# A bidirectional hybrid encoder layer on one core: strided moving operands of the dilated attention are copied by ScalarE into contiguous tiles first

## The chip, the core and the metric

The kernel is written for Trainium2 and runs on one core of one chip. The metric is device time in microseconds, as the median of several runs; the profile is one further execution under the hardware profiler. The core has five engines, each with its own instruction stream that it works through in order: PE (TensorE, the matrix multiplier; its weight loads are shown apart as PEld), DVE (VectorE), ACT (ScalarE), POOL (GpSimd) and SP (SyncE, which issues most DMAs). They wait for each other by semaphores.

## The reference, cut to what matters

One post-norm encoder layer over 2048 tokens of width 1024. Three mixers read one input projection: A, attention over dilated windows with 6 heads of 64; B, multi-head latent attention with 6 heads; C, chunked spatial gating. Their outputs are normalised and projected, and a squared-ReLU MLP follows. The change touches A alone:

```python
DILATED_PATTERNS = ((128, 1), (512, 4), (2048, 16))      # window, dilation

def _dilated_band_attention(q, k, v, window, dil, slopes):
    band = window // (2 * dil)                            # 64 for every pattern
    ...                                                   # tokens r, r+dil, r+2*dil, ... form one sequence
    s = jnp.einsum('brhnqc,brhnkc->brhnqk', qs, kw).astype(jnp.float32) * (Dh ** -0.5)
    bias = -(slopes[:, None, None, None] * (dil * jnp.abs(off)).astype(jnp.float32))
    s = jnp.where(valid, s + bias, NEG_INF)
    m = s.max(-1, keepdims=True)
    p = jnp.exp(s - m)
    den = p.sum(-1, keepdims=True)
    o = jnp.einsum('brhnqk,brhnkc->brhnqc', (p / den).astype(v.dtype), vw)
    ...
```

The three patterns of a head are then combined by the softmax of their log-sums.

## The kernel before, in words

The program has three parts: the latent columns of the input projection, a mixed part in which the latent attention `latent()` of B runs while "fillers" are woven into it one after the other, and the feed-forward. The fillers are `projection()`, then `dilated()` (its first matmul stands at 715.5 us of the profiled execution, its last value matmul at 1343.5 us), then the output projection. The loop in `mixers` decides by rates how many steps of a filler come after each step of `latent()`; inside that the framework's scheduler orders every engine's instructions for itself, by its own model of their durations and by priorities. So the order in which an engine works is fixed when the program is built.

A step of `latent()` is one 128-key tile of one block of 512 queries: three score matmuls of 512 columns into a bank `st` (L611 to L613), two exponentials of it on ACT (`pr` L618 and `ph` L619), a difference on POOL (`pl` L621), a sum on DVE (`ac` L636), and four steps later two value matmuls into `av` (L643, L644). A maximum runs ahead of it: matmul `mx` L593 and its reduction on DVE, L594. The three PSUM banks `st` are shared with the scores of `dilated()`, the four banks `mx` with its maxima and its sums.

`dilated()` treats head after head. `QA`, `QB`, `KA` and `KB` hold queries and keys of one head with the tokens along the free axis, in float32r, 4 bytes each. For dilation d the tokens of one residue lie d elements apart, so that the function `tok` cuts a slice with step 4 (pattern p = 1) or 16 (p = 2); for p = 0 it is contiguous. Per head there are 16 tiles of 128 tokens for each pattern, grouped in 20 units: 8 of p = 0, 8 of p = 1 (two tiles each) and 4 of p = 2 (four tiles each). For a tile three matmuls run: one for the maximum, a unit ahead for the next head (`amx`, L865: weights from QA, moving operand from KA), and two for the score (`ast`, L938 and L939: weights from KA and KB, moving operand from QA and QB). Both the weights and the moving operand are cut with the step. The moving operand has 256 columns, except that of the fourth tile of a unit of p = 2, which has 128. The maxima are read by DVE (`jk`, L870), the scores get their bias on DVE (`tt`, L947 to L961), an exponential on ACT (`apr`, L964), and a value matmul two units later (`aav`, L995).

The scheduling of `dilated()` has these constants: `D_LAG` = 2 (value matmuls two units behind the scores), `D_MAX` and `D_MRATE` (2.2 units of maxima for the next head with each score unit, from the fourth on), and priorities `HP`.

Of the kernel before, what the change touches and what calls it, by code (L numbers as in the profile page):

```python
# [12 lines left out]
F32 = mybir.dt.float32  # L13
F32R = mybir.dt.float32r
# [20 lines left out]
DILS = (1, 4, 16)  # L35
BIG = 1e30
OFFX = 60
RB = 3
ME = 3
LLAG = 4  # L40
U_STEP = 1
# [38 lines left out]
HP_DE = 0  # L80
HP_DV = 100
HP_DC = 0
HP = dict(L=HP_L, PG=HP_PG, PW=HP_PW, PE=HP_PE, LS=HP_LS, LE=HP_LE, LP=HP_LP, LM=HP_LM, LA=HP_LA, LV=HP_LV, LF=HP_LF, LQ=HP_LQ, LK=HP_LK, DM=HP_DM, DR=HP_DR, DS=HP_DS, DT=HP_DT, DE=HP_DE, DV=HP_DV, DC=HP_DC)
MS_C = None
MS_M = None
MS_F = None
# [13 lines left out]
def hybrid_layer(ctx: ExitStack, tc: tile.TileContext, a):  # L100
# [651 lines left out]
    def dilated():  # L752
# [3 lines left out]
        fp = sbuf(es, "af")  # L756
        dp = es.enter_context(tc.tile_pool(name="ad", bufs=2, space=DRAM))

        D = fp.tile([P, 256], F32, name="D")
        dma(D, a["dist"])  # L760

        KB = fp.tile([65, S], F32R, name="KB")
        pool.memset(f(KB[64:65]), 1.0)
# [1 line left out]
        def prep(h):  # L765
            hp, o = h // 2, (h % 2) * 64
            rows = slice(o, o + 64)
            s = dict(h=h)
            QA = qp.tile([P, S], F32R, tag="QA", name=f"QA{h}")
            QB = qp.tile([65, S], F32R, tag="QB", name=f"QB{h}")  # L770
            KA = qp.tile([P, S], F32R, tag="KA", name=f"KA{h}")
            s.update(QA=QA, QB=QB, KA=KA, KB=KB, V=[], bias=[])

            def load(c):
                cs_ = slice(c * 1024, (c + 1) * 1024)
                dma(QA[0:64, cs_], qa_d[hp][0][rows, cs_])
                dma(KA[0:64, cs_], ka_d[hp][0][rows, cs_])
                dma(QA[64:128, cs_], qa_d[hp][0][rows, cs_])
                dma(KA[64:128, cs_], ka_d[hp][1][rows, cs_])
                dma(QB[0:64, cs_], qa_d[hp][1][rows, cs_])  # L780

            s["parts"] = [lambda: load(0), lambda: load(1)]

            def rest():
                for p, d in enumerate(DILS):
                    bt = qp.tile([P, 256], F32, tag=f"bias{p}", name=f"bias{h}_{p}")
                    act.activation(bt, D, AF.Copy, scale=-8.0 * SLOPES[h] * d)
                    s["bias"].append(bt)
            s["parts"].insert(0, rest)

            def values(p):
                d = DILS[p]
                v = qp.tile([P, d, NT // d, 66], F32, tag=f"v{p}", name=f"v{h}_{p}", bufs=1)
                src = va_d[:, h * HD:(h + 1) * HD].rearrange("(n p r) c -> p r n c", r=d, p=P)
                pool.memset(v[:, :, :, 64:65], 1.0)
                for r in range(d if d == 4 else 1):
                    if d == 16:
                        dma(v[:, :, 0, 0:64], src[:, :, 0])
                    else:
                        dma(v[:, r, :, 0:64], src[:, r])  # L800
                s["V"].append(v.rearrange("p r n c -> p (r n) c")[:, :, 0:65])
            s["values"] = values
            s["mc"] = qp.tile([P, 3, 16], F32, tag="mc", name=f"mc{h}")
            s["u"] = 0
            return s

        def tok(ap, d, r, i0, n):
# [12 lines left out]
            return min(w0, S // DILS[p] - 256), 256, (j * pitch, j * pitch + 256)  # L820

        def cols(ap, p, tl, j):
            r, n, w0, w, o = tl[j]
            m0, m, (c0, c1) = wide(p, tl, j)
            if p == 2 and c1 - c0 > P:
                return ap.rearrange("p (i r) -> p r i", r=16)[:, r:r + 2, :]
            return tok(ap, DILS[p], r, m0, m)

        def bank_cols(ps, p, tl, j):
            m0, m, (c0, c1) = wide(p, tl, j)  # L830
            out = ps[:, c0:c1]
            return out.rearrange("p (r i) -> p r i", i=P) if p == 2 and c1 - c0 > P else out

        def at(p, tl, j):

# [18 lines left out]
                units.append((p, ts_[u:u + g], u))  # L854
        NU = len(units)

        def max_to(s, lim):
            while s["u"] < lim:
                u = s["u"]
                p, tl, base = units[u]  # L860
                d = DILS[p]
                ps = bank("mx", f"amx{s['h']}_{u}")
                with hp("DM"):
                    for j, (r, n, w0, w, o) in enumerate(tl):
                        pe.matmul(bank_cols(ps, p, tl, j), tok(s["QA"], d, r, n * P, P),  # L865
                                  cols(s["KA"], p, tl, j), start=True, stop=True, skip_group_check=True)
                    for j, (r, n, w0, w, o) in enumerate(tl):
                        col = {0: n, 1: n * 4 + r, 2: r}[p]
                        jk = ep.tile([P, 256], BF16, tag="jk", name=f"jk{s['h']}_{u}_{j}", bufs=1)
                        dve.tensor_tensor_reduce(jk[:, :w], ps[:, at(p, tl, j):at(p, tl, j) + w], s["bias"][p][:, o:o + w],  # L870
                                                 1.0, -3e38, ALU.add, ALU.max, s["mc"][:, p, col:col + 1])
                s["u"] = u + 1
                if s["u"] == NU:
                    max_done(s)
# [54 lines left out]
        def score(s, u):  # L929
            p, tl, base = units[u]  # L930
            d = DILS[p]
            h = s["h"]
            nm = f"{h}_{u}"
            st = bank("st", f"ast{nm}")
            with hp("DS"):
                for j, (r, n, w0, w, o) in enumerate(tl):
                    o_ = bank_cols(st, p, tl, j)
                    pe.matmul(o_, tok(s["KA"], d, r, n * P, P), cols(s["QA"], p, tl, j), start=True, stop=False, skip_group_check=True)  # L938
                    pe.matmul(o_, tok(s["KB"], d, r, n * P, P), cols(s["QB"], p, tl, j), start=False, stop=True, skip_group_check=True)  # L939
            tt = ep.tile([P, TB], F32, tag="tt", name=f"tt{nm}", bufs=2)  # L940
            pr = ep.tile([P, TB], F32, tag="pr", name=f"apr{nm}", bufs=D_LAG + 1)
            with hp("DT"):
                b = s["bias"][p]
                ws = [e[3] for e in tl]
                if p == 2:
                    rng = [(0, TB)]
                    dve.tensor_tensor(tt.rearrange("p (j w) -> p j w", w=P), st.rearrange("p (j w) -> p j w", w=P),  # L947
                                      b[:, None, 64:192].to_broadcast([P, 4, P]), op=ALU.add)
                elif ws == [256, 256]:
                    rng = [(0, TB)]  # L950
                    dve.tensor_tensor(tt.rearrange("p (j w) -> p j w", w=256), st.rearrange("p (j w) -> p j w", w=256),
                                      b[:, None, :].to_broadcast([P, 2, 256]), op=ALU.add)
                else:
                    rng = []
                    for j, (r, n, w0, w, o) in enumerate(tl):
                        x0 = at(p, tl, j)
                        if rng and rng[-1][1] == x0:
                            rng[-1] = (rng[-1][0], x0 + w)
                        else:
                            rng.append((x0, x0 + w))  # L960
                        dve.tensor_tensor(tt[:, x0:x0 + w], st[:, x0:x0 + w], b[:, o:o + w], op=ALU.add)  # L961
# [765 lines left out]
```

## Time and profile before

| | us |
|---|---|
| median of 3 runs (2996.32 to 3002.77) | 3000.21 |
| the profiled execution, by the same clock as the runs | 3006.01 |
| its span, from the first to the last instruction | 3004.2 |
| PE busy in the span | 2827.7 |
| DVE busy | 2149.7 |
| POOL busy | 1664.1 |
| ACT busy | 1332.7 |

The profiled execution is 5.8 us above the median. Each engine's busy time is the time in which at least one of its instructions was being worked on. Matmuls overlap: of a row that is shown with 0.40 us, the next one starts 0.23 us later, so what a matmul costs PE is read from the distance of two starts, not from its own duration. PEclk is the clock that PE was granted, as a share of full speed.

### The profile page before, as it was taken

To read this page: it belongs to the slowest core of one execution; us is meant where nothing else is said; L and a number is where in the kernel's file an instruction comes from. 1 tells how busy PE (TensorE), PEld (TensorE's weight loads), DVE (VectorE), ACT (ScalarE), POOL (GpSimd) and SP (SyncE) were. 2 spreads that over 40 slices of the span, in tenths; PEclk is the share of its full clock that TensorE was granted. 3 is DMA by queue.
4 is the path that set the end of the run, shared out by engine and by line. 5 is a ranking of instruction groups with operands and counts; after the bars stand their busy time and mean duration, and the time that the engine had idled before them with its cause. 6 is when DMAs were issued, how large, how long until landed. Compare 5 with 4: busy or idle time off the path is not lost. (4 is left out here: it accounts for less than half of the span.)

```text
span 3004.2 us, 38216 instructions
## 1 busy us (share of the span) xinstructions
PE 2827.7 (94%) x12556; PEld 2293.6 (76%) x12556; DVE 2149.7 (72%) x3519; ACT 1332.7 (44%) x2504; POOL 1664.1 (55%) x1251
## 2 busy tenths in 40 slices
PE   9999899999989999998999899989999999999996
PEld 7776777887777788886777688868887777777774
DVE  4246899887878988888867633383336777778899
ACT  4325555566544555465544434343434332222333
POOL 0115556567744554468755444454445765556667
PEclk9999999999999999998999999999999999999998
DMA  5345334236032444114365533333335322222222
GB/s 167 126 137 167 109 107 132 90 107 130 14 66 43 87 85 84 29 40 130 93 199 159 159 106 112 109 119 109 106 112 196 103 84 74 84 82 78 80 71 95
DMA packets 267760, 314.00 MB, mean 105 GB/s; under 512 B 91804, under 2 KB 157980, under 8 KB 267036
## 3 DMA queue, kind: packets, MB, share of 16 engines
q1 hardware_dynamic: 254248, 295.82, 33.0%
q10 hardware_dynamic: 13312, 15.73, 1.5%
q8 instruction: 99, 1.62, 0.2%
q14 instruction: 101, 0.83, 0.1%
HBM read 209.72 MB, written 98.60 MB: 103 GB/s over the span
## 5 line engine op out<-in xcount | busy, mean ns | idle before, releaser
L621 POOL TENSOR_TENSOR pl<-pr,ph 128x512 fp32r<-128x512 f32 x384 | 556.8, 1463 | 353.4 <-ACT ph L619 233.8
L636 DVE TENSOR_TENSOR ac<-ac,pr 128x512 f32<-128x512 f32 x312 | 359.2, 1151 | 45.4 <-ACT pr L618 38.3
L1571 DVE TENSOR_TENSOR acc<-o,acc 128x512 f32<-128x512 f32 x416 | 275.2, 683 | 110.6 <-PE o L151 108.4
L618 ACT ACTIVATE pr<-st 128x512 f32<-128x512 f32 x384 | 228.4, 597 | 232.0 <-PE st L613 209.2
L594 DVE TENSOR_REDUCE m<-mx 128x1 f32<-128x512 f32 x384 | 253.9, 681 | 40.3 <-PE mx L593 39.2
L619 ACT ACTIVATE ph<-st 128x512 fp32r<-128x512 f32 x384 | 224.0, 596 | 41.4 <-PE av L643 31.5
L643 PE MATMUL av<-ph,VV 128*128 128x512 f32 x384 | 161.2, 420 | 14.3 <-DVE y L658 14.3
L611 PE MATMUL st<-QH,KL 96*128 96x512 f32 x384 | 162.3, 423 | 12.1 <-ACT ph L619 12.1
L644 PE MATMUL av<-pl,VV 128*128 128x512 f32 x384 | 163.4, 426 | 6.0 <-POOL pl L621 5.5
L593 PE MATMUL mx<-KH,QH 96*128 96x512 f32 x384 | 157.5, 435 | 5.2 <-DVE m L594 1.9
L612 PE MATMUL st<-QL,KH 96*128 96x512 f32 x384 | 157.6, 410 | 0.0
L613 PE MATMUL st<-QH,KH 97*128 97x512 f32 x384 | 157.2, 412 | 0.0
L1499 DVE TENSOR_TENSOR t<-t,h 128x512 f32<-128x512 f32 x32 | 22.0, 686 | 142.8 <-PE h L151 132.0
L995 PE MATMUL aav<-apr,v 128*65 128x128 f32 (+3 forms) x624 | 115.5, 329 | 1.9 <-DVE mc L870 1.8
L870 DVE CUSTOM_DVE_ANT_0 jk<-amx,bias 128x256 bf16<-128x256 f32 (+2 forms) x288 | 103.3, 359 | 12.2 <-PE amx L865 4.6
L938 PE MATMUL ast<-QA,KA 128*128 128x256 f32 (+1 forms) x288 | 105.5, 371 | 4.6 <-DVE tt L961 4.3
L995 PEld LDWEIGHTS aav<-apr,v 128*65 128x65 f32 x624 | 82.5, 143 | 31.5 <-issue 2.7
L149 PE MATMUL po<-woh,y 128*128 128x512 f32 x256 | 103.8, 407 | 0.6 <-DVE xt L1310 0.3
L964 ACT ACTIVATE apr<-tt 128x192 f32<-128x192 f32 (+2 forms) x180 | 77.3, 467 | 60.9 <-PE aav L995 39.1
L150 PE MATMUL po<-woh,y 128*128 128x512 f32 x256 | 101.8, 399 | 1.7 <-DVE y L1233 1.7
L151 PE MATMUL po<-wol,y 128*128 128x512 f32 x256 | 100.6, 396 | 2.5 <-DVE wol L1192 2.5
L939 PE MATMUL ast<-QB,KB 65*128 65x256 f32 (+1 forms) x288 | 102.7, 368 | 0.0
(9014 smaller groups left out, 8722.6 us busy)
## 6 DMA issues: line engine op xcount, KB each, us to landing
A<-in_w SPq DMA_DIRECT2D x128, 256.0 KB, 2.7
hid_d<-t SPq DMA_DIRECT2D x128, 256.0 KB, 2.1
A<-hid_d SPq DMA_DIRECT2D x128, 256.0 KB, 3.0
B<-in_w_ff SPq DMA_DIRECT2D x64, 256.0 KB, 4.5
xr<-in_xT SPq DMA_DIRECT2D x56, 256.0 KB, 2.9
wr<-in_wf SPq DMA_DIRECT2D x48, 256.0 KB, 3.7
yr<-y_d SPq DMA_DIRECT2D x64, 128.0 KB, 2.5
xt<-in_x SPq DMA_DIRECT2D x32, 256.0 KB, 3.3
```

Of the source, the lines that this page charges most:

```text
L593: pe.matmul(ps, s["QH"][0:96, qt * P:(qt + 1) * P], kh[0:96, kc * TB:(kc + 1) * TB], start=True, stop=True)
L594: dve.tensor_reduce(s["m16"][:, qt, kc:kc + 1], ps, AX.X, ALU.max)
L611: pe.matmul(st, kl[0:96, kk], s["QH"][0:96], start=True, stop=False)
L612: pe.matmul(st, kh[0:96, kk], s["QL"][0:96], start=False, stop=False)
L618: act.activation(pr, st, AF.Exp, scale=SC)
L619: act.activation(ph, st, AF.Exp, scale=SC)
L621: pool.tensor_tensor(pl, pr, f(ph), op=ALU.subtract)
L636: (pool if kt in AC_POOL else dve).tensor_tensor(s["ac"], s["pr"] if kt == 1 else s["ac"], pr, op=ALU.add)
L643: pe.matmul(s["av"], VV[h][:, kt], ph, start=(kt == 0), stop=False)
L644: pe.matmul(s["av"], VV[h][:, kt], pl, start=False, stop=(kt == NT - 1))
L995: pe.matmul(s[key][0:65, c0:c0 + w], s["V"][p][:, units[u][2] + j], pr[:, a0:a0 + w], start=(first[key] == i), stop=(last[key] == i), skip ...
L1571: dve.tensor_tensor(t, ps, t, op=ALU.add)
```

## The change

Before a unit of p = 1 or p = 2 is computed, ScalarE copies the strided slice that serves as the moving operand into a contiguous tile of 512 columns (`straight`). One such tile holds one residue of p = 1 (which serves two units) or four residues of p = 2 (one unit). For the maxima it is the keys, `kc`, in one buffer (`KCB` = 1), copied when the first unit that needs it is emitted. For the scores it is the queries, `qac` and `qbc`, in two buffers each (`QCB` = 2), copied one unit ahead. The weights are still cut with the step from QA, KA and KB. That is 8 groups x 3 copies x 6 heads = 144 copies of 512 columns. To make room in SBUF, the value tiles of the three patterns share one tag with two buffers, the bias tiles are filled by a DMA for each head instead of from a resident tile `D` (and are half as wide for p = 2), and `RB` falls from 3 to 2 (the tiles `arb` that carry the reciprocals at the end of a head).

```diff
-RB = 3
+RB = 2
...
+KCB = 1
+QCB = 2
...
-                    bt = qp.tile([P, 256], F32, tag=f"bias{p}", name=f"bias{h}_{p}")
-                    act.activation(bt, D, AF.Copy, scale=-8.0 * SLOPES[h] * d)
+                    w0, w1 = (64, 192) if p == 2 else (0, 256)
+                    bt = qp.tile([P, w1 - w0], F32, tag=f"bias{p}", name=f"bias{h}_{p}")
+                    dma(bt, a["dist"][:, w0:w1])
+                    act.activation(bt, bt, AF.Copy, scale=-8.0 * SLOPES[h] * d)
...
-                v = qp.tile([P, d, NT // d, 66], F32, tag=f"v{p}", name=f"v{h}_{p}", bufs=1)
+                v = qp.tile([P, NT, 66], F32, tag="v", name=f"v{h}_{p}").rearrange("p (r n) c -> p r n c", r=d)
...
+        def straight(ap, p, g, tag, nm, bufs):
+            t = ep.tile([ap.shape[0], TB], F32R, tag=tag, name=nm, bufs=bufs)
+            if p == 1:
+                src, dst = tok(ap, 4, g, 0, TB), t
+            else:
+                src, dst = ap.rearrange("p (i r) -> p r i", r=16)[:, 4 * g:4 * g + 4], t.rearrange("p (r i) -> p r i", r=4)
+            act.copy(dst, src)
+            return t
...
+        def keys_of(s, u):
+            p = units[u][0]
+            g = group(p, u)
+            if g is not None and s.get("kg") != (p, g):
+                s["kg"] = p, g
+                with hp("DK"):
+                    s["kc"] = straight(s["KA"], p, g, "kc", f"kc{s['h']}_{u}", KCB)
+
+        def queries_of(s, u):
+            p = units[u][0]
+            g = group(p, u)
+            if g is not None and (p, g) not in s["qc"]:
+                with hp("DQ"):
+                    s["qc"][p, g] = (straight(s["QA"], p, g, "qa", f"qac{s['h']}_{u}", QCB),
+                                     straight(s["QB"], p, g, "qb", f"qbc{s['h']}_{u}", QCB))
...
+                keys_of(s, u)
...
-                        pe.matmul(bank_cols(ps, p, tl, j), tok(s["QA"], d, r, n * P, P),
-                                  cols(s["KA"], p, tl, j), start=True, stop=True, skip_group_check=True)
+                        pe.matmul(dst_cols(ps, p, tl, j), tok(s["QA"], d, r, n * P, P),
+                                  piece_of(s["kc"], p, tl, j) if p else cols(s["KA"], p, tl, j), start=True, stop=True, skip_group_check=True)
...
+            queries_of(s, u)
+            if u + 1 < NU:
+                queries_of(s, u + 1)
...
-                    pe.matmul(o_, tok(s["KA"], d, r, n * P, P), cols(s["QA"], p, tl, j), start=True, stop=False, skip_group_check=True)
-                    pe.matmul(o_, tok(s["KB"], d, r, n * P, P), cols(s["QB"], p, tl, j), start=False, stop=True, skip_group_check=True)
+                    qa, qb = ([piece_of(t, p, tl, j) for t in s["qc"][p, group(p, u)]] if p else
+                              [cols(s[t], p, tl, j) for t in ("QA", "QB")])
+                    pe.matmul(o_, tok(s["KA"], d, r, n * P, P), qa, start=True, stop=False, skip_group_check=True)
+                    pe.matmul(o_, tok(s["KB"], d, r, n * P, P), qb, start=False, stop=True, skip_group_check=True)
```

The scheduler orders the program anew from the second half of the projection to the start of the output projection; ahead of it and behind it every engine's instructions stand as they stood. Two places show what comes to lie between what.

PE, maxima of the first head, the units 15 to 17 (p = 1 ends with unit 15, p = 2 begins with 16). The last two numbers of a name are unit and buffer; `amx` are maxima, `st` scores and `av` values of the latent attention. Before:

```order
L865 MATMUL amx_15_7142<-KA_6750,QA_6748 128x256 x2
L611 MATMUL st_2_5_7405<-QH_2_6405,KL_1896 128x512
L612 MATMUL st_2_5_7405<-QL_2_6406,KH_1895 128x512
L613 MATMUL st_2_5_7405<-QH_2_6405,KH_1895 128x512
L865 MATMUL amx_16_7164<-KA_6750,QA_6748 128x256 x3
L865 MATMUL amx_16_7164<-KA_6750,QA_6748 128x128
L865 MATMUL amx_17_7177<-KA_6750,QA_6748 128x256 x3
L865 MATMUL amx_17_7177<-KA_6750,QA_6748 128x128
```

And in the changed program:

```order
L903 MATMUL amx_15_7151<-kc_14_7142,QA_6746 128x256 x2
L648 MATMUL av_1_6964<-pl_1_15_7296,VV_4832 128x512
L615 MATMUL st_2_5_7422<-QH_2_6405,KL_1896 128x512
L616 MATMUL st_2_5_7422<-QL_2_6406,KH_1895 128x512
L617 MATMUL st_2_5_7422<-QH_2_6405,KH_1895 128x512
L903 MATMUL amx_16_7175<-kc_16_7173,QA_6746 128x256 x3
L903 MATMUL amx_16_7175<-kc_16_7173,QA_6746 128x128
L903 MATMUL amx_17_7190<-kc_17_7188,QA_6746 128x256
```

The matmuls are the same, but each group of maxima now reads a `kc` of its own, and since there is one buffer, the copy of the next `kc` has to lie between the last `amx` of one group and the first of the next. Four matmuls of 512 columns stand between units 15 and 16, and none between 16 and 17.

ACT, maxima of the third head and scores of the second, from the exponentials of unit 12 (`apr_12`) to those of the latent attention's step 5 (`pr_0_5`). Before:

```order
L964 ACTIVATE apr_12_8241<-tt_12_8240 128x192
L964 ACTIVATE apr_12_8241<-tt_12_8240 128x256
L618 ACTIVATE pr_0_5_8410<-st_0_5_8406 128x512
L619 ACTIVATE ph_0_5_8411<-st_0_5_8406 128x512
L618 ACTIVATE pr_0_6_8426<-st_0_6_8422 128x512
```

And in the changed program:

```order
L1007 ACTIVATE apr_12_8287<-tt_12_8286 128x192
L1007 ACTIVATE apr_12_8287<-tt_12_8286 128x256
L862 COPY kc_17_8227<-KA_7631 128x512
L862 COPY qac_17_8504<-QA_6746 128x512
L862 COPY qbc_17_8506<-QB_6747 65x512
L862 COPY kc_18_8242<-KA_7631 128x512
L622 ACTIVATE pr_0_5_8466<-st_0_5_8462 128x512
L623 ACTIVATE ph_0_5_8467<-st_0_5_8462 128x512
L622 ACTIVATE pr_0_6_8482<-st_0_6_8478 128x512
```

Four copies stand ahead of the latent attention's exponential, and the last of them has to wait until PE has done the maxima of unit 17, which read the copy that is first of the four.

## Rows read from the trace of the kernel before

**Rows 1.** The page: busy us (share of the span) and instructions of each engine.

```profile
PE 2827.7 (94%) x12556; PEld 2293.6 (76%) x12556; DVE 2149.7 (72%) x3519; ACT 1332.7 (44%) x2504; POOL 1664.1 (55%) x1251
```

**Rows 2.** Busy time by stretch: stretch, length, engines, granted clock.

```profile
core 0: us, PE busy (x) PEld busy (x) DVE busy (x) ACT busy (x) POOL busy (x), PEclk, DMA share, GB/s
780.00:880.00 100.00, 88.06 (x392) 71.56 (x392) 80.00 (x195) 45.86 (x96) 54.46 (x40) 0.90 0.13 24
...
980.00:1080.00 100.00, 95.68 (x492) 81.15 (x491) 93.31 (x207) 52.45 (x108) 53.88 (x43) 0.98 0.40 84
...
1014.00:1072.00 58.00, 55.84 (x260) 47.45 (x258) 55.02 (x143) 28.87 (x64) 32.73 (x26) 1.00 0.18 38
715.00:1345.00 630.00, 592.03 (x2834) 495.87 (x2835) 537.01 (x1224) 328.17 (x667) 353.45 (x269) 0.94 0.31 63
```

**Rows 3.** PE's waits from 715 to 1345 us: total, times, longest.

```profile
PE st L611 <- ACT ph L619: 11.3, 4, 7.1
PE ast L938 <- DVE tt L961: 4.3, 5, 1.5
```

**Rows 4.** Timeline of PE, scores of p = 0: start, duration, instruction.

```profile
1004.20 0.28 PE L938 MATMUL ast<-QA,KA 128*128 128x256 f32 x1
1004.31 0.29 PE L939 MATMUL ast<-QB,KB 65*128 65x256 f32 x1
1004.43 0.29 PE L938 MATMUL ast<-QA,KA 128*128 128x256 f32 x1
```

**Rows 5.** Timeline of PE, a 512-column matmul, scores of p = 1, and another.

```profile
1034.64 0.40 PE L643 MATMUL av<-ph,VV 128*128 128x512 f32 x1
1034.88 0.40 PE L938 MATMUL ast<-QA,KA 128*128 128x256 f32 x1
1035.10 0.42 PE L939 MATMUL ast<-QB,KB 65*128 65x256 f32 x1
1035.34 0.42 PE L938 MATMUL ast<-QA,KA 128*128 128x256 f32 x1
1035.57 0.42 PE L939 MATMUL ast<-QB,KB 65*128 65x256 f32 x1
1035.81 0.42 PE L644 MATMUL av<-pl,VV 128*128 128x512 f32 x1
```

**Rows 6.** Timeline, end of a score unit of p = 2: matmuls and their weight loads.

```profile
1063.08 0.39 PE L939 MATMUL ast<-QB,KB 65*128 65x256 f32 x1
1063.10 0.31 PEld L938 LDWEIGHTS ast<-QA,KA 128*128 128x128 f32 x1
...
1063.30 0.29 PE L938 MATMUL ast<-QA,KA 128*128 128x128 f32 x1
1063.32 0.31 PEld L939 LDWEIGHTS ast<-QB,KB 65*128 65x128 f32 x1
1063.40 0.40 PE L939 MATMUL ast<-QB,KB 65*128 65x128 f32 x1
...
1063.53 0.21 PEld L611 LDWEIGHTS st<-QH,KL 96*128 96x128 f32 x1
1063.62 0.43 PE L611 MATMUL st<-QH,KL 96*128 96x512 f32 x1
1063.66 0.19 PEld L612 LDWEIGHTS st<-QL,KH 96*128 96x128 f32 x1
```

**Rows 7.** Groups by form, 780 to 1345 us: the 128-column scores; busy, mean ns.

```profile
L939 PE MATMUL ast<-QB,KB 65*128 65x128 f32 x24 | 9.3, 386 | 0.0
...
L938 PE MATMUL ast<-QA,KA 128*128 128x128 f32 x24 | 7.1, 295 | 0.0
```

**Rows 8.** Instructions of 512 columns: two contiguous, one strided (ns min/median/max).

```profile
L974 ACT COPY acc<-aav 65x512 f32<-65x512 f32 x18 | 10.4, 578 | 2.5 <-PE aav L995 2.5
...
L658 DVE TENSOR_TENSOR y<-av,y x24: 648/676/684, 330.5 to 1508.5; 64x512 f32<-64x512 f32 x24
...
L983 DVE TENSOR_TENSOR acc<-aav,acc x48: 1040/1077/1127, 862.1 to 1347.2; 65x512 f32<-65x512 f32 x48
```

**Rows 9.** Timeline: ACT releases a bank, and PE's next weight load starts.

```profile
1041.46 0.59 ACT L619 ACTIVATE ph<-st 128x512 fp32r<-128x512 f32 x1
...
1042.10 0.31 PEld L938 LDWEIGHTS ast<-QA,KA 128*128 128x128 f32 x1 [0.73 <-ACT ph L619]
```

**Rows 10.** DMA issues (KB, median us to landing) and POOL's wait for one.

```profile
v<-va_d SPq DMA_DIRECT2D x12, 512.0 KB, 7.0
v<-va_d SPq DMA_DIRECT2D x24, 128.0 KB, 4.8
arb<-ard SPq DMA_DIRECT2D x24, 128.0 KB, 2.9
...
POOL acc L1017 <- DMA arb<-ard: 13.0, 4, 6.2
```

## What was predicted before the changed kernel ran

> **What bounds the kernel now.** The page's busy times come first: PE 94% of the span, DVE 72%, ACT 44% [rows 1]. The change touches only the dilated stage, so the next view is busy time by stretch. From 715 to 1345 us PE is busy 592 of 630 us, DVE 537, POOL 353, ACT 328 [rows 2]. PE sets the pace; DVE is close behind, at 93% between 980 and 1080 us; ACT has about half its time free. PE's waits there are short, the longest total being 11.3 us for the exponential `ph` that frees a bank `st` [rows 3]. The granted clock averages 0.94 over the stage and 0.90 in its emptiest stretch [rows 2]: the stretch where PE stands idle most also runs slowest.
>
> Then the timeline, for what a matmul costs PE from start to start. A score of p = 0 (contiguous, 256 columns) takes 0.115 us (1004.20 to 1004.43 for two, [rows 4]), the same with step 4 0.2325 (1034.88 to 1035.81 for four), and a contiguous 512-column matmul as much (0.24, [rows 5]). A 256-column score with step 16 takes 0.22 (from 1063.08 to 1063.30, [rows 6]). So a strided score costs twice a contiguous one, and the plain reading is that contiguous copies give half of it back.
>
> **What the change takes from PE.** The plain reading leaves out that the weights stay strided. The last tile of a unit of p = 2 shows what that costs, because its moving operand has only 128 columns. The weight load for L939 starts at 1063.32, just after L938 of 128 columns began at 1063.30; L938 would be done in half of 0.22, and L939 is indeed recorded as starting at 1063.40, but the load that follows starts only at 1063.53, 0.21 after its forerunner, and L939 lasts 0.40 where L938 lasts 0.29 [rows 6]. It is not one case: over all 24 such pairs the means are 386 and 295 ns [rows 7]. A contiguous load is followed by the next after 0.13 us (1063.53 to 1063.66, [rows 6]). I read this as: a strided weight load takes about 0.215 us (1063.10 to 1063.53 for two), whatever matmul runs beside it, and a matmul behind it can't start sooner. The Trainium skill, "SBUF — State Buffer", Specifications (TRN2), says that full bandwidth needs two hits or more in a 16-byte line of SBUF. The trace agrees for steps of 16 and 64 bytes, moving operand and weights alike; it has no smaller step.
>
> So the gain goes by what follows. Where a strided matmul of p = 1 is followed by another with strided weights, 0.2325 becomes 0.215; where a foreign matmul with contiguous weights follows, 0.2325 becomes 0.115. In the new order 93 of the 288 matmuls of p = 1 are of the second kind and 195 of the first: 93 x 0.1175 + 195 x 0.0175 = 10.9 + 3.4 = 14.3 us. For p = 2, 0.215 stays, except for 13 wide ones ahead of a foreign matmul: 13 x 0.1 = 1.3. Sum **-15.6 us**, all of it on PE. The bounds: -12 if the loads of p = 1 themselves take 0.2325, and -55 if weight loads never bound (288 x 0.1175 + 216 x 0.1). I take -15.6 because the 24 pairs are the only rows with a short matmul between strided loads. DVE, the next late engine, at 93% between 980 and 1080 us, may take part of that gain back there.
>
> **What the copies cost ACT.** No strided copy by ACT stands in this trace. A contiguous one of 512 columns takes 578 ns. The nearest strided rows are DVE's: 1077 ns for a sum with a strided operand against 676 contiguous, 401 more [rows 8]. So 0.58 to 0.98 us. I take 0.98: PE's moving reads, its weight loads and DVE all slow with these steps, and I see no reason why ACT's reads should not. 144 copies are then 141 us (84 at the low end) in about 630. ACT hides them on average, 328 + 141 of 630 being 74%, but not evenly: all 24 copies of a head fall into its last two thirds. From 1014 to 1072 us ACT is busy 28.9 of 58 us [rows 2]; 24 x 0.98 = 23.5 more make 90% (74% with 0.58).
>
> **The round trip of `kc`.** With one buffer, a copy waits for the last `amx` of the group before, and the first `amx` of its own waits for the copy. The trip is: the tail of the last matmul beyond its slot, 0.28 - 0.115 = 0.165 [rows 4]; a signal to ACT; the copy; a signal to PE, 0.05 (`ph` ends at 1042.05, the load starts at 1042.10, [rows 9]; I take the same for the other way); the weight load, 0.215. That is 0.48 + 0.98 = 1.46 us (1.06 with the cheap copy). What PE has to do meanwhile is counted in the new order, with 0.235 for 512 columns: of 48 copies one has nothing (units 16 and 17 of the first head), two have one matmul, 8 have four (0.94 us), 6 have five (1.17), two have six (1.40), the other 29 more than 1.46. Uncovered: 1.46 + 2 x 1.225 + 8 x 0.52 + 6 x 0.285 + 2 x 0.06 = **+9.9 us** (3.7 with the cheap copy). The copies `qac` and `qbc` have 5 us or more of PE's work ahead of their first use in every case, so they cost PE nothing directly.
>
> **What waits behind the copies.** ACT works in order. Behind a copy stand `pr` and `ph`, and for them wait the banks `st` (PE), the sum `ac` (DVE) and the difference `pl` (POOL). PE already loses 11.3 us to late `ph` with ACT half idle [rows 3]. Where four copies stand in a row ahead of `pr`, they are 3.9 us, and the last waits for PE besides. From both sides: nothing, if the banks and the value matmuls four steps behind cover it; or, if ACT at 90% loses another sixth of the 58 us to waits inside its order, it needs 106% of the stretch, 3.5 us a head over what there is; with as much again for DVE, which waits for `pr`, 7 us, 42 for six heads. I take **+14 us**, rather more than what PE loses today to `ph`, since ACT's load rises from 50% to 90% in these stretches, and a third of the upper bound.
>
> **The small edits.** The 18 bias DMAs are issued three units ahead of their use, and the value tiles, now in two shared buffers, with the first score of their pattern; the slowest of these loads takes 7.0 us [rows 10] and the value matmuls come two units later, some 9 us (120 units between 780 and 1345 us). So I put them at 0; cover gone, each would show once a head, up to 7 us. `RB` = 2 lets the third `arb` (2.9 us, [rows 10]) start only after the first product; POOL already waits 13.0 us for these and is busy 353 of 630 us, so I put it at 0 (2 us a head without cover). SP's queue holds 17 more DMAs in all (18 for the biases, one less for `D`), and behind each of them waits only what SP issues next.
>
> **Sum.** -15.6 + 9.9 + 14 = +8 us. The profiled execution (3006.0 us, span 3004.2) is 5.8 above the median; the difference is carried over to the median: 3000.2 + 8 = **3008 us**, 0.27% slower. A measurement of this kernel tells a difference of about 0.2%, 6 us.
>
> **The rivals.**
> *Covered, or nearly: no change.* The loss behind the copies is 5 us instead of 14, because the scheduler has put work there: -15.6 + 9.9 + 5 = -1, 3000 us. For it: the waits in rows 3 are few. Against: the scheduler can have planned with the shorter copy only.
> *The copy costs 0.58 us: faster.* Then the round trips cost 3.7, ACT stays at 74% and what waits behind the copies costs 1: -15.6 + 3.7 + 1 = -11, 2989 us. It decides at a copy of about 0.7 us.
> *Weight loads don't bound: much faster.* Each strided matmul falls to 0.115 us: -55 + 9.9 + 5 = -40, 2960 us. The Trainium skill, "TensorE: Matmul & The Clock Gate", "Step-by-step: what each phase is for", gives PE two independent read ports and says that the next weights load while a matmul runs, so that a matmul costs its columns. By that rule this case; the 24 pairs [rows 7] speak against it for strided weights.
> *ACT becomes the pacer: slower by more.* The 106% above, with the clock falling in the gaps as in the stretch with 0.90 [rows 2]: -15.6 + 9.9 + 42 = +36, 3036 us. It decides where ACT's busy share in the p = 1 and p = 2 part of a head passes 90%.
>
> **How the numbers follow.** Forecast (3008) 0.34; no change (3000) 0.31; cheap copy (2989) 0.20; loads don't bound (2960) 0.07; ACT the pacer (3036) 0.08. Faster by over 0.2%: 0.27; within: 0.31; slower: 0.42. The range leaves out the 2960 case, most of the pacer and the fringe of the cheap copy: 2981 to 3027. The forecast's own range is 3006 to 3020.
>
> **What the changed profile would show.** Starts of scores of p = 1 and p = 2 0.21 to 0.22 apart, the last of a group 0.115 ahead of its follower; at 0.115 throughout, the third rival is right. Copies `kc`, `qac`, `qbc` near 0.98 us; near 0.58, the second is. A new wait "PE amx for ACT kc" of about 10 us in all, about 1.5 the longest. ACT near 74% from 715 to 1345 us and near 90% in the last two thirds of a head; PE's wait for `ph` and DVE's for `pr` longer. I am wrong if the stage is shorter than 620 us or the new wait is absent. Nothing should move ahead of the projection's second half, nor behind the start of the output projection.

## The result and the profile after

The changed kernel takes 3019.5 us (median of 6 runs, 3018.0 to 3025.3), the one before 3001.5 beside it. The medians are 18.0 us apart; the ratio on record is 1.0069, 95% interval 1.0055 to 1.0082, which is 21 us (17 to 25), so 0.6 to 0.7% slower. The profiled execution is the longest of the six (3025.31 us, against 3006.01 before), so the two traces differ by 19.3 us. From the first `amx` to the end of the last `aav`, at 1369.5 us, the dilated stage takes 649.1 us, before 630.8: 18.3 us longer, and that is nearly the whole difference. (Before, the last value matmul ends at 1346.4 us; what stands at 1343.5 belongs to the unit ahead of the last.) The first fence is from the page (busy us, share, instructions; [rows 1] before), the second is busy time over the stage without its last 2.3 us (answers to [rows 2]).

```profile
PE 2824.9 (93%) x12556; PEld 2284.5 (76%) x12556; DVE 2156.9 (71%) x3519; ACT 1471.2 (49%) x2648; POOL 1663.5 (55%) x1251
```

```profile
720.40:1367.20 646.80, 590.87 (x2828) 488.91 (x2829) 537.32 (x1223) 462.67 (x802) 350.86 (x266) 0.94 0.30 63
```

ACT has 135 us more to do in the stage than [rows 2] shows, the others as much as before: only the engine with time to spare got more work. PE's busy time didn't fall either, and its idle gaps from the first `amx` to the last `aav` rose from 37.4 to 55.9 us. The next view is PE's waits, 715 to 1380 us (total, times, longest; [rows 3] before):

```profile
PE amx L903 <- ACT kc L862: 18.9, 15, 6.6
PE ast L981 <- ACT ph L623: 4.7, 6, 1.5
PE amx L903 <- DVE mc L908: 3.5, 4, 1.8
...
PE av L648 <- POOL pl L625: 2.7, 5, 1.4
...
PE st L615 <- ACT ph L623: 1.2, 1, 1.2
```

The new wait is there, at the top. Its longest piece is none of the copy's: it ends at 849.24, where ACT has stood 6.96 us for a DMA (`KH`, L545, waits for `kr`), and the copy of `kc` comes right behind. In the kernel before the same stand of ACT showed as 7.1 us of "st for ph" [rows 3]. So some 12 us of the 18.9 are new. The waits of all engines over the same stretch show who else has to do with ACT (`pl`, `pr` and `ac` are the latent attention's, as above):

```profile
POOL pl L625 <- ACT ph L623: 180.1, 83, 6.9
ACT pr L622 <- PE st L617: 66.4, 62, 4.7
DVE ac L640 <- ACT pr L622: 33.5, 29, 6.3
...
ACT bias L791 <- DMA bias<-in_dist: 21.3, 8, 6.6
```

Before, ACT waited 161.1 us for PE's scores ("ACT pr for PE st"), DVE 30.6 for `pr`, and POOL 173.9 for `ph`. That ACT now waits 66.4 us for PE's scores, not 161.1, says that it is more often behind PE than before. The copies themselves, by their line (min/median/max ns, first and last start), with what ACT waited for ahead of them:

```profile
L862 ACT CAST qac<-QA x48: 1061/1112/1182, 725.2 to 1354.8; 128x512 fp32r<-128x512 f32 x48
L862 ACT CAST kc<-KA x48: 1056/1104/1187, 728.2 to 1262.0; 128x512 fp32r<-128x512 f32 x48
L862 ACT CAST qbc<-QB x48: 1048/1101/1143, 789.1 to 1355.7; 65x512 fp32r<-65x512 f32 x48
its engine sat idle before it (us, times) until:
  PE ast L981: 11.3, 14
  PE amx L903: 9.2, 11
```

A strided copy takes 1.10 us, 144 of them 159 us (an instruction's record overlaps with the next one's, so ACT's busy time rises by less, 135 us); and ACT stands another 20.5 us until PE has read the old content of the tile. One round trip of `kc` in the timeline (start, duration; in brackets the idle time ahead and who ended it):

```profile
1056.13 0.40 PE L903 MATMUL amx<-kc,QA 128*128 128x256 f32 x1
...
1056.36 0.39 PE L615 MATMUL st<-QH,KL 96*128 96x512 f32 x1
...
1056.69 1.07 ACT L862 CAST kc<-KA 128x512 fp32r<-128x512 f32 x1
...
1057.06 0.40 PE L648 MATMUL av<-pl,VV 128*128 128x512 f32 x1
...
1057.82 0.49 PE L903 MATMUL amx<-kc,QA 128*128 128x256 f32 x1 [0.36 <-ACT kc L862]
```

From the start of the last reader of the old tile to that of the first reader of the new one it is 1.69 us, of which four 512-column matmuls cover most: 0.36 us of PE's idle time are left. The prediction's 1.46 us is counted from the end of the last reader's slot (here 1056.36) and holds the weight load; here 1.46 us are over when that load begins. Last, a group of scores of p = 1 on PE and, in a fence of its own, its weight loads from the second on; [rows 5] has such a group before:

```profile
938.85 0.28 PE L981 MATMUL ast<-qac,KA 128*128 128x256 f32 x1
938.96 0.39 PE L982 MATMUL ast<-qbc,KB 65*128 65x256 f32 x1
939.20 0.40 PE L981 MATMUL ast<-qac,KA 128*128 128x256 f32 x1
939.43 0.40 PE L982 MATMUL ast<-qbc,KB 65*128 65x256 f32 x1
939.67 0.39 PE L647 MATMUL av<-ph,VV 128*128 128x512 f32 x1
```

```profile
938.85 0.31 PEld L982 LDWEIGHTS ast<-qbc,KB 65*128 65x128 f32 x1
939.06 0.33 PEld L981 LDWEIGHTS ast<-qac,KA 128*128 128x128 f32 x1
939.30 0.33 PEld L982 LDWEIGHTS ast<-qbc,KB 65*128 65x128 f32 x1
```

One of the four steps is short (0.11 us), the other three are 0.235, as far apart as the weight loads. Over all groups that stand between 512-column matmuls at full clock, with what the matmul behind them is held up, four scores of p = 1 take 0.824 us where they took 0.947, a pair of maxima of p = 1 0.351 where it took 0.476, and eight scores of p = 2 1.67 where they took 1.63. The own time of all matmuls of p = 1 (from start to next start, without idle time, at either clock) is 65.2 us where it was 70.5, that of p = 2 59.4 where it was 59.3.

### The profile page after: what moved, and what is told of

Same layout as the page of the kernel before. It is cut to its first block, busy times and chain, and to the rows that moved or that the text cites. A ratio compares the mean times of both kernels' runs of the same rounds, so it can differ in the third digit from the quotient of the medians.

```text
span 3023.5 us, 38465 instructions
## 1 busy us (share of the span) xinstructions
PE 2824.9 (93%) x12556; PEld 2284.5 (76%) x12556; DVE 2156.9 (71%) x3519; ACT 1471.2 (49%) x2648; POOL 1663.5 (55%) x1251
## 5 line engine op out<-in xcount | busy, mean ns | idle before, releaser
L640 DVE TENSOR_TENSOR ac<-ac,pr 128x512 f32<-128x512 f32 x312 | 366.0, 1173 | 51.2 <-ACT pr L622 44.0
L647 PE MATMUL av<-ph,VV 128*128 128x512 f32 x384 | 160.9, 419 | 11.5 <-DVE y L662 11.4
L615 PEld LDWEIGHTS st<-QH,KL 96*128 96x128 f32 x384 | 76.9, 200 | 27.3 <-ACT ph L623 9.4
L647 PEld LDWEIGHTS av<-ph,VV 128*128 128x128 f32 x384 | 77.4, 202 | 26.7 <-DVE y L662 14.2
```

The costliest lines, as they stand in the source:

```text
L615: pe.matmul(st, kl[0:96, kk], s["QH"][0:96], start=True, stop=False)
L640: (pool if kt in AC_POOL else dve).tensor_tensor(s["ac"], s["pr"] if kt == 1 else s["ac"], pr, op=ALU.add)
L647: pe.matmul(s["av"], VV[h][:, kt], ph, start=(kt == 0), stop=False)
```

## The experiments

The scheduler orders the stage anew for nearly every edit, so a time also holds what the new order is worth. Two pairs, both in the fifth experiment, have every engine's instructions in the same order: the kernel before and `mcont_before`, and `wcont_before` and `both_before`. How far the order may go shows in the fourth.

The granted clock differs too. Over the 97 runs of the twelve kernels below, a run with 0.001 less of it than its kernel's mean is 1.8 us longer (correlation -0.70). The means go from 0.9615 (`kcpool`) over 0.9695 (the changed kernel) and 0.970 to 0.971 (before) to 0.9735 (`cheap`) and 0.974 (`wcont_before`). Whether an order brings its clock, or the clock came by itself, no run here tells, so differences of a few us between kernels are not split further.

**1. Which part of the change costs?** `small` has the small edits without any copy; `unread` makes all 144 copies, but the matmuls read the strided slices as before; `cheap` takes the copies from contiguous slices, so that the copy is shorter and the columns are other ones.

```diff
 # small: no copies, strided operands
-                keys_of(s, u)
...
-            queries_of(s, u)
...
 # small and unread
...
-                    qa, qb = ([piece_of(t, p, tl, j) for t in s["qc"][p, group(p, u)]] if p else
-                              [cols(s[t], p, tl, j) for t in ("QA", "QB")])
+                    qa, qb = [scols(s[t], p, tl, j) for t in ("QA", "QB")]
 # cheap
-                src, dst = tok(ap, 4, g, 0, TB), t
+                src, dst = ap[:, g * TB:(g + 1) * TB], t
...
```

> The changed kernel without its copies: the strided slices are read by PE as before, and only the small edits stay (RB = 2, value tiles in two shared buffers, biases loaded by a DMA for each head). If copies and round trips cost the time (the theory), this run lies within 4 us of before, 2997 to 3006. Rival 1, the small edits cost it (ACT stands still 21 us for bias DMAs in the changed profile): 3010 to 3020. Rival 2, it is the new order alone: anything between, with the matmul spacing of before.

> The 144 copies are made, but no matmul reads them: PE reads the strided slices as before, so no matmul waits for a copy and no copy waits for a matmul. ACT's load is that of the changed kernel (about 460 us in the stage). If ACT's load delays the exponentials and that is the main loss, 3012 to 3025 (no matmul gain, load in full). If the round trip through the single kc is the main loss, the load being covered, 3000 to 3008. If the small edits are it, as long as the run with these alone.

> The changed kernel, but the copies read contiguous slices of the same tensors, so PE gets the wrong columns of the moving operand and the values are not the layer's; count, size, buffers and waits of the copies are those of the changed kernel. Theory: a contiguous copy takes 0.6 us instead of 1.10, ACT's share in the stage falls from 72% to about 60%, the waits for kc fall from 18.9 to about 8 us, and the run lies 8 to 16 us under the changed kernel, 3003 to 3011. If the copy's duration doesn't matter (order, or the small edits), within 4 us of the changed kernel's 3019.

Measured, against 3001.3 us before on the same chip: `small` 2998.4, ratio 0.9986 (0.9966 to 1.0006); `unread` 3031.3, 1.0110 (1.0090 to 1.0129); `cheap` 2992.0, 0.9975 (0.9959 to 0.9991). No cost of the small edits shows (10 us less to 2 more). The copies alone, read by nobody and so in nobody's round trip, cost 27 to 39 us in an order of their own, more than the 3012 to 3025 us expected. With short copies the change makes the kernel 3 to 12 us faster than before, also past the 3003 to 3011 us expected; by the slope above, its higher clock (0.9735 against 0.970 beside it) goes with up to 7 of these. First fence: waits of all engines in `unread`, 715 to 1380 us, with PE's longest; the second is its copy and two of `cheap`; the third PE's wait for `kc` in `cheap`.

```profile
POOL pl L625 <- ACT ph L623: 186.1, 88, 13.1
...
DVE ac L640 <- ACT pr L622: 41.9, 41, 3.8
...
PE st L615 <- ACT ph L623: 17.0, 13, 3.7
```

```profile
L874 ACT CAST kc<-KA x48: 1050/1124/1226, 730.8 to 1236.8; 128x512 fp32r<-128x512 f32 x48
...
L862 ACT CAST qac<-QA x48: 603/621/642, 722.7 to 1327.3; 128x512 fp32r<-128x512 f32 x48
L862 ACT CAST kc<-KA x48: 612/620/640, 724.7 to 1237.4; 128x512 fp32r<-128x512 f32 x48
```

```profile
PE amx L903 <- ACT kc L862: 8.6, 5, 6.2
```

In `unread` the exponentials `ph` and `pr` come late for everyone who waits for them: PE 17.0 us in 13 waits where [rows 3] has 11.3 in 4, one of which was the DMA's. In `cheap` the wait for `kc` is, but for the DMA's 6.2 us, 2.4. From 1.10 to 0.62 us a copy, ACT has 70 us less to do, and the kernel takes 27 us less.

**2. Do the weight loads bound the groups?** The changed kernel, with the weights of p = 1 and p = 2 cut as contiguous slices too; they hold other columns.

```diff
-                    pe.matmul(o_, tok(s["KA"], d, r, n * P, P), qa, start=True, stop=False, skip_group_check=True)
+                    pe.matmul(o_, s["KA"][:, base_of(p, tl, j):base_of(p, tl, j) + P], qa, start=True, stop=False, skip_group_check=True)
...
```

> The changed kernel, but the weights of the dilated scores and maxima are contiguous slices of QA, KA and KB, so the values are not the layer's; everything else as in the changed kernel. If strided weight loads bound these matmuls (the theory), a group of four scores of p = 1 falls from 0.82 us to about 0.48 and one of eight of p = 2 from 1.67 to about 0.85, some 30 us less of PE's time in the stage, of which 10 to 30 show: 2990 to 3009. If something else bounds them (the write into PSUM, the signals), the groups stay at 0.82 and 1.67 and the time at 3019.

Measured: 3002.2 us, 1.0008 (0.9995 to 1.0022). The timeline of PE, scores of a unit of p = 2:

```profile
1049.56 0.28 PE L985 MATMUL ast<-qac,KA 128*128 128x256 f32 x1
1049.68 0.29 PE L986 MATMUL ast<-qbc,KB 65*128 65x256 f32 x1
1049.81 0.28 PE L985 MATMUL ast<-qac,KA 128*128 128x256 f32 x1
...
1050.30 0.22 PE L985 MATMUL ast<-qac,KA 128*128 128x128 f32 x1
1050.36 0.28 PE L986 MATMUL ast<-qbc,KB 65*128 65x128 f32 x1
```

Now every step is 0.12 us, and the short ones 0.06 to 0.11. Eight scores take 0.95 instead of 1.67 us, four of p = 1 0.48 instead of 0.82. That the strided weights bound the groups in the changed kernel is shown. Outside its gaps PE needs 42 us less in the stage than in the changed kernel, and the program is 17 us shorter: PE's gaps rose from 55.9 to 79.3 us, those that ACT ended from 24.8 to 35.3. The wait for `kc` is the longest of them.

```profile
PE amx L907 <- ACT kc L866: 24.4, 20, 6.6
PE av L648 <- POOL pl L625: 10.6, 16, 1.9
PE st L615 <- ACT ph L623: 9.0, 8, 1.7
```

**3. Does the load or its kind set the price?** `unread_cheap` is `unread` with the short copies; `p1only` makes and reads the copies of p = 1 alone, 72 of 144.

```diff
 # p1only
-                keys_of(s, u)
+                if p == 1:
+                    keys_of(s, u)
...
```

> 144 copies that no matmul reads, from contiguous slices, so 0.62 us each instead of 1.11; PE reads strided slices as before. It gives a second point for what ACT's load costs without any gain and any round trip. In proportion to ACT's time (89 against 160 us): 30 x 0.56 = 17, 3012 to 3021. If a threshold decides: 2998 to 3006.

> Copies for p = 1 only, one kc: 72 of them, about 79 us of ACT. The matmuls of p = 2 read strided slices as before; by the weight load they lose nothing (their groups of eight took 1.63 us strided and 1.67 copied). PE keeps its whole gain, 46 groups x 0.12 + 47 x 0.125 = 11 us. If ACT's load costs in proportion, half of 30 us: net +4, 3000 to 3010. If only the stretches in which ACT is nearly full cost, much less than half: 2988 to 2997.

Measured, against 2999.4 us before: `unread_cheap` 3014.2, 1.0048 (1.0030 to 1.0067); `p1only` 3005.1, 1.0013 (1.0000 to 1.0027). ACT's added time of 89 us (144 x 0.62) costs 14 us unread, 160 us cost 33: the price grows with the time that ACT is given, and its rival, a threshold (2998 to 3006 us for `unread_cheap`), is refuted. Two points in different orders don't show that it is in proportion. And it is no fixed price: `cheap` has the same 89 us as `unread_cheap` and is 22 us shorter, more than the reading of contiguous operands brings on PE. Where the scheduler puts a copy that others wait for, and where one that nobody waits for, may differ too; how much of the 22 us that is, and how much is order or clock, no run settles.

**4. Does the single `kc` buffer cost?** A second one doesn't fit beside `RB` = 2, so `RB` = 1 is run alone and with `KCB` = 2.

```diff
 # rb1 and rb1_kcb2
-RB = 2
+RB = 1
 # rb1_kcb2
-KCB = 1
+KCB = 2
```

> The changed kernel with one tile for the reciprocals (RB = 1), the control for the next run, for which SBUF has no room otherwise. The stores at the end of a head become serial; POOL and SP have time. Every theory: 3017 to 3026.

> As rb1, with two buffers for kc, so that a copy no longer waits for the maxima of the group just before it. If the round trip through the one kc costs what was forecast (10 us), 7 to 15 us under rb1 and the wait of PE for kc falls from about 19 to under 9 us. If ACT's load alone is the cost (the copies that nobody reads cost 30 us by themselves), within 4 us of rb1, since PE then waits elsewhere for the same late ACT.

Measured: `rb1` 3010.4, 1.0038 (1.0021 to 1.0054); `rb1_kcb2` 3018.6, 1.0064 (1.0043 to 1.0084). PE's first waits, 715 to 1380 us, of the one and of the other:

```profile
PE amx L903 <- ACT kc L862: 18.4, 15, 6.3
PE ast L981 <- ACT ph L623: 6.7, 6, 2.0
```

```profile
PE st L615 <- ACT ph L623: 12.7, 7, 6.8
PE ast L981 <- ACT ph L623: 8.2, 4, 6.7
```

With two buffers the wait for `kc` is gone, 21 us of waits for `ph` stand where `rb1` has 11, and the program is no shorter: 8 us longer, where a round trip with a cost of its own would have made it 7 to 15 shorter. So that cost doesn't show; PE waits for another of ACT's outputs instead. It is not excluded, for the two kernels differ in order and clock (0.972 and 0.969), and each trace is of the kernel's shortest run (2999.5 and 3004.7 us). `rb1`, with fewer buffers, is some 9 us shorter than the changed kernel, outside the 3017 to 3026 us that every theory had. Its order and its clock (0.972 against 0.9695) differ; what else could make it shorter is not known. Differences below 10 us between kernels of different order are not put down to anything here.

**5. What is the gain without its price?** The kernel before, without any copy, with moving operands, weights, or both cut as contiguous slices (other columns than the pattern's).

```diff
 # mcont_before and both_before
...
-            return tok(ap, DILS[p], r, m0, m)
+            return ap[:, r * (S // DILS[p]) + m0:r * (S // DILS[p]) + m0 + m]
 # wcont_before and both_before
-                    pe.matmul(o_, tok(s["KA"], d, r, n * P, P), cols(s["QA"], p, tl, j), start=True, stop=False, skip_group_check=True)
+                    pe.matmul(o_, s["KA"][:, base_of(p, tl, j):base_of(p, tl, j) + P], cols(s["QA"], p, tl, j), start=True, stop=False, skip_group_check=True)
...
```

> The kernel before, but the moving operands of p = 1 and p = 2 are cut as contiguous slices of QA, QB and KA, without any copy; the slices hold other columns than the pattern's, so the computed values are other ones. This is the gain of the change without its price. Theory (the strided weights bound what contiguous operands can give back; the change gains about 11 us of PE and loses about 30 by ACT's load): 2985 to 2992 us, four scores of p = 1 in 0.82 us, eight of p = 2 in 1.63 to 1.67. Rival 1 (the gain of 15.6 or more was there and was lost to waits that the copies make): 2975 to 2985. Rival 2 (weights don't bound): four scores in 0.47 and about 2960 us.

> The kernel before with its strided moving operands, but with weights of p = 1 and p = 2 cut as contiguous slices, which hold other columns than the pattern's. Theory (either strided operand alone holds a matmul of 256 columns at 0.2325 us): four scores of p = 1 stay at 0.93 to 0.95 us, and the time at 2994 to 3003 us. Rival (the strided weight load alone makes the spacing of 0.2325, the moving operand reads at full speed): four scores in 0.47 to 0.6 and 2950 to 2975 us.

> The kernel before with both moving operands and weights of p = 1 and p = 2 cut as contiguous slices, without copies; they hold other columns than the pattern's. This is what the strides cost in all. Theory: four scores of p = 1 in 0.47 to 0.49 us, eight of p = 2 in 0.93 to 0.96, PE busy 40 to 55 us less in the stage; of this a part goes into waits for POOL and ACT, so 2955 to 2980 us. Rival (another engine bounds the stage once PE is relieved): PE's gaps take nearly all, 2985 to 3000 us.

Measured, against 2996.7 us before: `mcont_before` 2995.1, 0.9992 (0.9980 to 1.0003); `wcont_before` 2987.7, 0.9969 (0.9952 to 0.9986); `both_before` 2971.2, 0.9904 (0.9870 to 0.9937). Busy time over the stage of each, in this order, each to within 0.4 us of its last `aav` (before, in full: 630.8 us, PE busy 593.4):

```profile
717.40:1341.50 624.10, 581.50 (x2844) 488.00 (x2844) 538.75 (x1226) 328.99 (x670) 352.65 (x269) 0.95 0.31 63
...
716.90:1328.60 611.70, 570.03 (x2840) 463.96 (x2840) 540.81 (x1224) 328.43 (x668) 351.71 (x268) 0.98 0.32 65
...
718.90:1319.60 600.70, 540.52 (x2838) 434.50 (x2839) 538.42 (x1224) 329.31 (x668) 354.33 (x269) 0.95 0.33 66
```

`mcont_before` has every engine's instructions in the order of before. Its groups are as short as the changed kernel's (0.823 us for four scores of p = 1, 1.67 for eight of p = 2), and yet it gains nothing that can be told from no change: between 6 us less and 1 more. That is less gain than either the theory (2985 to 2992 us) or its rival had. PE's busy time in the stage falls by 11.6 us, 6.8 of them the own time of p = 1 (70.5 to 63.7 us); PE is at half clock (0.5 granted) for 58 us there, before for 72. PE's gaps rose from 37.4 to 42.6 us; those that DVE ended, from 19.1 to 24.2. `wcont_before` keeps four scores of p = 1 at 0.928 us, so either strided operand alone holds a matmul back; its 9 us are more than the 2994 to 3003 us expected allow, its order is a new one, and PE is at half clock for only 24 us of its stage. `both_before` halves the groups (0.48 and 0.95 us): PE's busy time in the stage falls by 53 us, the stage by 30, for DVE now ends 40.4 of PE's 60.2 us of gaps and is busy 538 of 601 us, 90%. The time is inside the 2955 to 2980 us expected, but the gaps are DVE's, not POOL's and ACT's.

The second pair of one order gives the plainest figure here. `both_before` is `wcont_before` with contiguous moving operands, and 16.5 us shorter, each of its runs (2964.9 to 2978.1) below each of the other's (2980.8 to 2999.9). So the same edit of the moving operands gives 16.5 us beside contiguous weights and some 2 us beside strided ones.

**6. Would another engine make the copies cheaper?** The 48 copies of `kc` on POOL.

```diff
-            act.copy(dst, src)
+            if tag == "kc":
+                pool.tensor_copy(dst, src)
+            else:
+                act.copy(dst, src)
```

> The changed kernel with its 48 copies of kc made by POOL; the 96 of qac and qbc stay with ACT. Theory (what costs is ACT's time, some 0.18 us for each us of copies): 53 us off ACT give back 9.5, so about 3010 us, if POOL with its 351 of 647 us takes the copies free; each us of POOL's priced alike would take it all back, 3019. Rival (the round trip through the single kc buffer costs by itself): a slower copy by POOL makes PE's wait for kc longer than 18.9 us and the time 3022 us or more.

Measured: 3064.5 us, 1.0213 (1.0187 to 1.0240), the slowest of all. The copies by their line, and what POOL waited for ahead of them; then busy time over the stage:

```profile
L863 POOL CAST kc<-KA x48: 1027/1091/1577, 725.3 to 1297.8; 128x512 fp32r<-128x512 f32 x48
its engine sat idle before it (us, times) until:
  PE amx L906: 43.7, 17
...
  PE amx L906: 1.7, 3
```

```profile
719.30:1407.30 688.00, 614.25 (x2841) 499.03 (x2842) 552.08 (x1225) 418.82 (x758) 407.11 (x315) 0.91 0.29 60
```

The copy costs POOL what it costs ACT, 1.09 us; PE waits for it only 1.7 us in all (the last line, under who waited for it). But POOL stands 43.7 us ahead of its copies until PE has read the single buffer, and behind them stand the differences and sums of the latent attention. The stage is 39 us longer than in the changed kernel. 18 of these are PE's gaps (73.8 us against 55.9), of which DVE ended 37.8, ACT 26.1 and POOL itself 6.1; 21 are PE's busy time, with 122 us at half clock against 75. The theory's price (3010 to 3019 us) is refuted. The rival's time (3022 us or more) came, but not by its wait, which is 1.7 us. That POOL's stand is what reaches PE through DVE and ACT is likely, but not followed through the trace.

## Why the prediction was right, and where it was not

The forecast was 3008 us and slower, the kernel is slower at 3019.5: inside the range, and at the edge of the forecast's own. The mechanism was right in two points, the bound by the weight loads and a cost by ACT's copies above the gain. The sum was not: that it is 11.5 us off lies with the gain, of which 15.6 us were forecast and about 2 show. The two costs, forecast at 24 us, came to 20 to 23 (18 to 21 of loss and 2 of gain); that is luck in part, since experiment 4 does not bear out how they are split.

- **The strided weights bound the groups: right.** Experiment 2 shows it, and the third rival (2960 us) is refuted with it. The Trainium skill, "TensorE: Matmul & The Clock Gate", "Step-by-step: what each phase is for", says that the next weights load while a matmul runs. The loads do run beside the matmuls here, but only the contiguous ones are done in time: 0.12 us a step in `wcont`, 0.235 in the changed kernel.
- **The gain on PE, -15.6: too high.** The weight loads of p = 1 take 0.235 us apart, not the 0.215 that was read off p = 2. This is the lower bound of the prediction, -12, or less: the groups measured give 46 x 0.123 for the scores and 47 x 0.125 for the maxima, 11.5 us, if all stood at full clock between 512-column matmuls, and p = 2 loses just under 1; by its own time p = 1 gains 5.3 us in the changed kernel and 6.8 in `mcont_before`. The short step stands behind the first matmul of a group, not ahead of its follower; the sum is the same.
- **That PE's gain is gain of time: wrong in the main.** `mcont_before` has the same short groups and shortens the program by about 2 us (6 less to 1 more). The prediction said in half a sentence that DVE may take part of it back, and put no number there. That was the step with the most to lose: a PE that is busy 94% is still not the only one who sets the pace.
- **The copy, 0.98 us: too low,** at 1.10. The choice of the upper end was right, the end itself was not one: ACT's strided read costs 0.5 us over its contiguous one (1.10 against 0.62), where DVE's 0.4 [rows 8] was taken for the limit. The prediction's two copies, 0.58 and 0.98, lay 19 us apart for 58 us of ACT's time; by that slope the 17 us more of copies are 6 us more.
- **The round trip of `kc`, +9.9: the wait is there, a cost of its own doesn't show.** Some 12 us of new waits, 14 of 0.2 to 1.9 us (forecast: 18 of up to 1.46). But without them nothing is gained in experiment 4. Perhaps they were counted beside the lateness of ACT, of which they are a part; the two orders differ, so this is not shown.
- **What waits behind the copies, +14: not measured by itself.** `unread`, with the load and no round trip, has 33 us, more than both costs together in the changed kernel. In the profile PE's waits for `ph` are 5.9 us, before 11.6; without the stand of 7.1 us that now shows at `kc` they were 4.5, so they rose a little. DVE's wait for `pr` rose from 30.6 to 33.5 us and POOL's for `ph` from 173.9 to 180.1, as forecast in direction; POOL's rise is hardly more than what the 3% longer stage makes.
- **ACT's load:** 72% of the stage (463 of 647 us), forecast 74. In the last two thirds of a head 69 to 80%, not 90, since 27 of the 144 copies lie outside these stretches. ACT is never the pacer, and the change loses all the same; the fourth rival's point of 90% was not where it began.
- **The small edits: right** at nothing that shows (`small`). ACT does stand for the bias DMAs, 21.3 us in the changed kernel and 15.8 in `small`, and the time of `small` doesn't show it.
- **The cheap copy, 2989 us: right as a rival,** at 2992 with copies of 0.62 us, but not by its sum, which has the gain at 15.6.

What stays open is the sum of the measured parts: -2 for the gain and +33 for the load make +31, the whole has +21. And `cheap`, whose copies still take ACT's time, is 3 to 12 us shorter than before, where contiguous operands without any copy gave 2. The orders differ, `rb1` and the changed kernel lie 9 us apart without a known cause, and the clocks differ; no run tells whether that is all.

## What to carry to other kernels

A contiguous copy of one operand of a short matmul gains little while the other operand is still strided (2 us here, against 16.5 with both): look at the weight loads' starts before making it, and ask for both or for neither. Both strides together cost 19 to 39 us here (`both_before`), which is about what another layout of queries and keys could give without copies. The free time of an engine that works in order is not free: 144 copies that nobody read cost 27 to 39 us on an ACT that was busy 71% of the stage with them. A copy that waits for its buffer also holds up everything queued behind it (20.5 us on ACT, 43.7 on POOL), and the reader's own waits don't show that.

## What the runs showed of the hardware

- ACT copies 512 float32 columns in steps of 16 or 64 bytes in 1.10 us, contiguous ones in 0.62 (`cheap`); POOL's strided copy takes 1.09 (`kcpool`).
- Weights of 128 columns load every 0.235 us with a step of 16 bytes and every 0.22 with one of 64 (changed kernel); a 256-column matmul on contiguous operands takes 0.12 (`wcont`, `both_before`), each at full clock.
- Contiguous weights alone leave p = 1 at 0.232 us a matmul (`wcont_before`), contiguous moving operands alone at 0.235 but for one short step in a group (`mcont_before`), and both strided at 0.2325 [rows 5]: the two don't add up, the slower one counts.
